# Sliding-window attention by pairs of chunks: one run of logits in six PSUM banks, and keys turned four chunks at a time by DMA

## The chip, the cores and the metric

The kernel runs on one core of one Trainium2 chip. The core has a matrix engine (TensorE, PE in the profile; PEld is its loading of the stationary operand), a vector engine (DVE), a scalar engine (ACT), GpSimd (POOL) and a queue engine (SP) that issues nearly all DMA transfers. TensorE writes to PSUM, which has eight banks of 128 partitions x 512 float32; DVE and ACT read them. The metric is the device time of one execution in microseconds (us); a kernel's time is the median of its runs.

## The reference

One layer of a hybrid decoder on x (2048 tokens x 1024 channels, float32). The tokens are cut into 16 chunks of 128.

```python
proj = einsum('bsd,de->bse', rms_norm(x, norm_w), w_in)      # 1024 -> 2816 columns
rq, rk, rv, rg, sq, sk, sv, sg = split(proj)                 # retention, then attention
ro = group_norm(retention(rotary(rq), rotary(rk), rv)) * silu(rg)
so = sliding_window_attention(sq, sk, sv, ...) * silu(sg)
x + einsum('bse,ed->bsd', concatenate([ro, so]), w_out)
```

The attention has 8 query heads and 2 key heads of 64 channels. Queries and keys are RMS-normed per head. A token attends to the 128 tokens up to itself, so a chunk of queries meets its own keys and those of the chunk before:

```python
logits = einsum('bnqhgd,bnkhd->bhgnqk', qb, kband) * HD ** -0.5
logits = where(mask, logits + bias, -1e30)                   # bias by distance and head
probs = softmax(concatenate([logits, sink]))[..., :-1]       # one learned sink per head
out = einsum('bhgnqk,bnkhd->bnqhgd', probs, vband)
```

The retention runs over the same chunks with a state that is passed on from chunk to chunk.

## The kernel before

*Products.* The two projections are four streams of block products (`products`, L754): three over columns of w_in (512, 384 and 512 wide), and one over w_out. A stream multiplies blocks by a scheme with seven products in place of eight for two-by-two blocks, for eight pairs of chunks: 56 products. A product is 12 matmuls into one bank ("acc"): each operand is split into a high and a low part in a faster format ("x" and "w"; `split`, L569), and three combinations of the parts are summed over four blocks of 128 rows. ACT makes the high part and DVE the low one. A finished product leaves its bank by a copy on ACT or an addition on DVE (tiles s, t, u, r, c).

*Attention* runs beside the second and third stream. `window` (L1188) goes through the chunks, and `attend` (L1323) does one of them. DVE scales queries ("qn") and keys ("kn"). The queries are turned by `turn_by_dma` (L484): ACT splits the 32-bit words into two planes of 16-bit halves ("apart"), SP stores them to DRAM ("planes_dram") and a transposing DMA brings them back turned ("qT"). The keys are turned by one transpose on TensorE against the identity ("ident,kn"), and ACT writes them, scaled, into "ks", a tile that holds the keys of a chunk, of the one before and of the one after, laid out so that a band of 160 keys is a contiguous slice. The logits of one head and 32 queries are one matmul of 64 rows x 32 columns against 160 keys; a chunk has 32 of them (eight heads by four groups of 32 queries), each of which the profile counts as two matmuls, so 64, in two operations of 32 counted matmuls, each with two banks (L1384 to 1397). DVE adds bias and finds the row's extreme ("lg<-m,bias,nsnk", two for a bank), ACT takes the exponential and its sum, and DVE turns the weights in blocks of 32 x 32 ("pT<-lg"). `values` (L1227) multiplies them with the values for two chunks at once, 144 counted matmuls of 32 x 64 into four banks, which ACT copies out ("so").

*Retention* (L907) follows with 17 steps of matmuls of 64 x 64, and the gates and the fourth stream after it.

*What sets the order.* Nothing here is ordered by hand. Every operation is recorded with its engine, an assumed duration and a due time (`Program.op`, L147). `emit` (L176) then runs a list scheduler: it keeps a clock for each engine, picks the operation that can start first and breaks ties by due time, and fixes the order of each engine's instructions. Because one helper records all of them, nearly every row of the profile has line L421, and the tiles' names tell the operations apart. Due times count products: stream 1 is 0 to 56, stream 2 is 56 to 112 and so on. Chunk c's attention is due at `WIN[0] + c * WIN[1]`, retention's at `RET`, the gates' at `GATE`. The planner has costs for a change of tile size on TensorE (`CHANGE`, `LESSER`), for the fetch of its instructions (`PIECE`, `ASKED`, `LONG`), and limits: `CAP` (buffers of each kind; "bank" is 8), `SHARE` (buffers for each use; block products may take 3 banks, everything else 6), `AHEAD` and `AHEAD_OF` (how early a load, or the split of an x or w block, may be issued). `HELD` lists intermediate tiles that stay in SBUF and are neither stored to DRAM nor loaded again; `TURNED` lists the chunks whose tiles are turned by DMA.

The two operations of logits for one chunk:

```python
for t in range(2):
    ...
    op(f32(160, 2), go, [qT, ks_t], pls[2 * t : 2 * t + 2], due + 0.5 + 0.3 * t, "eighths", label="logits", many=64)
```

Of the kernel before, what the change touches and what calls it, by code (L numbers as in the profile page):

```python
# [39 lines left out]
P = 128  # L40
# [63 lines left out]
LATER, CROWD, MOST, SOONER = 0.5, 0.0, 7, 62.0  # L104
# [239 lines left out]
HELD = {"sums": ((3, 1), (5, 4), (5, 5), (6, 3), (6, 6), (7, 0), (7, 1), (7, 5)), "ro": (1, 4, 8, 9, 10, 12, 13, 14, 15), "q": (0, 3, 13, 14), "gates": (1, 7), "so": (2, 14, 15)}  # L344
# [49 lines left out]
VALUES = {"T": (2.26, 2.48, False)}  # L394
# [30 lines left out]
def layer(ctx, tc, xt, xfirst, xtok, nw, w_in, w_rn, qkw, sinks, biasg, rope, decays, dmask, gpow, w_out, out):  # L425
# [113 lines left out]
    planes_dram = [scratch([P, 1024], f"planes{n}_dram", NCH, U16) for n in range(4)]  # L539
# [648 lines left out]
    def window(at):  # L1188
# [22 lines left out]
        ks_t = kb("ks", "att")  # L1211
        op({"G": (0.3, 0.4, True)}, lambda e: e.memset(ks_t()[:, 0:P], 0.0), [], [ks_t], at(0) - 4, label="no keys")
        held = []
        for c in range(NCH):
            i = c >= 2 * FIRST_PAIRS
            a, b = held_q.get(c), sb("akv", [P, P])
# [3 lines left out]
            load(b, aq_dram[1][c], at(c) - 4, 64, of=lambda t: t[:, :P])  # L1220
            fac = Part(qk_batches[i][1], lambda t, k=c - 2 * FIRST_PAIRS * i: t[:, k, :])
            held.append(attend(c, a, b, fac, qk_batches[i][1], at(c), bias_t[c > 0], ks_t, nsnk))
            if c % 2:
                values(c - 1, held, at(c))
                held = []

# [47 lines left out]

    def qk_sums(p, row, col, b, due):
# [47 lines left out]
    def attend(c, a, b, fac, facs, due, bias_t, ks_t, nsnk):  # L1323
        slot = c % 2
        qn, kn = kb("qn", "att"), sb("kn", [P, P])
# [9 lines left out]
        if c in HELD["q"] and c in TURNED["q"]:  # L1335
# [4 lines left out]
        op(  # L1340
            {"V": (0.22, 0.3, True)},
            lambda e: e.tensor_tensor(
                kn().rearrange(hd, d=HD), b().rearrange(hd, d=HD), fac()[:, 8:10].unsqueeze(2).to_broadcast([P, KVH, HD]),
                ALU.mult,
            ),
            [b, facs], [kn], due, label="kn",
        )

        pk, pq = ps(), ps()
        op(  # L1350
            turns(1), lambda e: e.transpose(pk()[:, 0:P], kn(), ident()), [kn, ident], [pk], due + 0.2, "small",
            label="turn k", many=2,
        )
# [13 lines left out]
        def go(e):  # L1367

            b4 = ks_t().rearrange("p (b t) -> p b t", t=P)
            e.activation(  # L1370
                b4[:, 1:3, :] if slot == 0 else b4[:, 0:4:3, :],
                pk()[:, 0:P].unsqueeze(1).to_broadcast([P, 2, P]), AF.Copy,
                scale=wqk(),
            )

        op({"A": act(256, 0.09)}, go, [pk, wqk], [ks_t], due + 0.3, label="ks")


        if c % SUMMED == 0:
            sums_of[:] = [sb("nm", [P, SUMMED, AH]), sb("den", [P, SUMMED, AH]), [], []]  # L1380
        nm, den, nms, dens = sums_of
        lgs = [wide("lg") for _ in range(KVH)]

        pls, weights_of = [ps() for _ in range(4)], {}  # L1384
        for t in range(2):

            def go(e, t=t):
                for j in range(2):
                    for u, q in enumerate(QUARTERS):
                        for g, r in enumerate((L, H)):  # L1390
                            o = (2 * t + j) * P + u * 32
                            e.matmul(
                                pls[2 * t + g]()[q, j * 160 : j * 160 + 160], qT()[r, o : o + 32],
                                ks_t()[r, slot * 256 + u * 32 : slot * 256 + u * 32 + 160], start=True, stop=True,
                            )

            op(f32(160, 2), go, [qT, ks_t], pls[2 * t : 2 * t + 2], due + 0.5 + 0.3 * t, "eighths", label="logits", many=64)
        for bank, heads in enumerate([(2 * t + j, g) for j in range(2)] for t in range(2) for g in range(2)):
            later, n = due + 0.5 + 0.2 * bank, len(heads)
            pl, g = pls[bank], heads[0][1]  # L1400
            lg = lgs[g]
            out = Part(lg, lambda t, i=heads[0][0]: t[:, i * 160 : (i + 2) * 160])

            part = lambda x, k=bank: x[:, c % SUMMED, k // 2 * 4 + k % 2 : k // 2 * 4 + 4 : 2]
            nmp, denp = Part(nm, part), Part(den, part)
            nms.append(nmp)
            dens.append(denp)

            def go(e, pl=pl, out=out, heads=heads):
                for j, (i, g) in enumerate(heads):  # L1410
                    h, o = 2 * i + g, slice(j * 160, j * 160 + 160)
                    e.tensor_tensor_reduce(
                        out()[:, o], pl()[:, o], bias_t[i]()[:, g * 160 : g * 160 + 160],
                        1.0, nsnk()[:, h : h + 1], ALU.add, ALU.min, nm()[:, c % SUMMED, h : h + 1],
                    )

            op(
                {"V": (0.312 * n, 0.312 * n + 0.13, False)}, go, [pl, nsnk, *(bias_t[i] for i, _ in heads)], [out, nmp],
                later, label="bias", also=(nm, lg),
            )  # L1420

            def go(e, out=out, heads=heads):
                for j, (i, g) in enumerate(heads):
                    h, o = 2 * i + g, slice(j * 160, j * 160 + 160)
                    e.activation(
                        out()[:, o], out()[:, o], AF.Exp, scale=-1.0, bias=nm()[:, c % SUMMED, h : h + 1],
                        accum_out=den()[:, c % SUMMED, h : h + 1],
                    )

            op(  # L1430
                {"A": (0.417 * n, 0.417 * n + 0.14, False)}, go, [out, nmp], [out, denp], later + 0.2, "exp", label="exp",
                also=(nm, den, lg),
            )
            weights_of[bank] = out
        pTs = []
        for g in range(KVH):
            if slot == 0:
                wholes[g] = wide("pT")
# [144 lines left out]

WIN = (58.5, 4.8)
RET = (124.5, 2.15)
GATE = (139.0, 5.65)

LEAD = 7.0  # L1590


_SHAPES = {
# [92 lines left out]
```

## Time and profile before

| | us |
|---|---|
| median of three runs (676.03 to 679.65) | 676.88 |
| the profiled execution | 673.99 |
| its span | 672.2 |
| TensorE busy | 663.9 |
| DVE busy | 589.9 |
| ACT busy | 475.6 |
| logits matmuls, 1024, summed | 21.7 |
| values matmuls, 1152, summed | 26.5 |
| key transposes on TensorE, 16, summed | 4.1 |

Matmuls are pipelined, so the busy time of a group and the duration of one of its members say little of what it costs on the path; that is read from the starts of the work around it, in order of time. Rows of that view have the start, the time to the end of the last of a row, the engine, the line, the operation, the tiles written and read, the array's tile size, the shape and the count; "[0.58 <-ACT ks L421]" is idle time before the row and what ended it. In a view by stretches the columns are the stretch, its length, the busy time of PE, PEld, DVE, ACT and POOL with the number of instructions, the granted TensorE clock, the busy share of the DMA engines and GB/s.

### The profile page before, as it was taken

What the parts mean: (1) busy time and instruction counts of PE and PEld (TensorE: products, weight loads), DVE (VectorE), ACT (ScalarE), POOL (GpSimd) and SP (SyncE); (2) the same over time, 40 slices, a digit from 0 to 9 for tenths busy, and PEclk for the clock granted to TensorE, in tenths of its full rate; (3) what the DMA queues carried; (4) which work ended last, traced back from release to release, by engine and by line L of the source; (5) the groups of instructions that cost most, each with busy time, mean ns of one, the idle gap of its engine ahead of it and who ended that gap; (6) DMA issues with size and microseconds to landing.
All of it is one profiled execution on the core that took longest, in us unless ns stands there. A gap on an engine that the chain in (4) does not pass through costs nothing.

```text
span 672.2 us, 16349 instructions
## 1 busy us (share of the span) xinstructions
PE 663.9 (99%) x5948; PEld 560.2 (83%) x5948; DVE 589.9 (88%) x1369; ACT 475.6 (71%) x1147; POOL 16.7 (2%) x39
## 2 busy tenths in 40 slices
PE   9999999999999999999999999999999999999998
PEld 7888888889999999898887777688888888888886
DVE  6999967887899978899998998989998999987782
ACT  7662788657898764889889987989999844533300
POOL 0000000034100000000000000000000000000000
PEclk9999999999999999999999999999999999999999
DMA  8976699988887999999989887989998685025652
GB/s 315 362 245 228 190 363 301 334 281 293 239 205 214 284 240 280 321 274 325 262 227 255 209 259 232 257 257 226 275 260 245 192 201 198 1 79 196 213 186 95
DMA packets 154144, 161.65 MB, mean 240 GB/s; under 512 B 67792, under 2 KB 95312, under 8 KB 154064
## 3 DMA queue, kind: packets, MB, share of 16 engines
q1 hardware_dynamic: 153920, 160.60, 79.5%
q8 instruction: 47, 0.77, 0.5%
q14 instruction: 33, 0.27, 0.1%
q10 hardware_dynamic: 144, 0.00, 0.0%
HBM read 97.05 MB, written 49.35 MB: 218 GB/s over the span
## 4 chain that ended last, share of the span: by engine, by line
PE 87%; DMA 4%; DVE 4%; ACT 3%; issue 1%; SPq 1%; ACTq 0%; DVEq 0%
PE acc L421 79%; PE m L421 8%; DMA planes_dram<-apart 2%; SPq L421 1%; DVE w L421 1%; DVE x L421 1%; DMA x<-s_dram 1%; DMA w<-in_w_in 0%; DMA ro_dram<-ro 0%; DMA g_dram<-c 0%; ACT qk L421 0%; ACT so L421 0%; ACT ro L421 0%; ACT apart L421 0%; DVE state L421 0%
## 5 line engine op out<-in xcount | busy, mean ns | idle before, releaser
L421 PE MATMUL acc<-w,x 128*128 128x512 f32 (+1 forms) x2700 | 591.5, 377 | 1.8 <-DVE x L421 0.9
L421 PEld LDWEIGHTS acc<-w,x 128*128 128x128 f32 x2700 | 491.5, 188 | 88.5 <-issue 6.0
L421 DVE TENSOR_TENSOR x<-x 128x512 fp32r<-128x512 f32 (+2 forms) x220 | 143.4, 672 | 15.8 <-ACT x L421 12.7
L421 ACT ACTIVATE x<-x 128x512 fp32r<-128x512 f32 (+1 forms) x187 | 111.3, 617 | 29.9 <-DVE x L421 16.7
L421 DVE TENSOR_TENSOR w<-w 128x512 fp32r<-128x512 f32 (+3 forms) x96 | 61.1, 656 | 3.4 <-ACT w L421 3.3
L421 ACT ACTIVATE lg<-lg,nm 128x160 f32<-128x160 f32 x128 | 53.1, 421 | 6.8 <-DVE nm L421 6.7
L421 ACT ACTIVATE w<-w 128x512 fp32r<-128x512 f32 (+1 forms) x72 | 40.9, 603 | 14.0 <-DVE w L421 4.0
L421 DVE SCALAR_TENSOR_TENSOR w<-w,nw_sb 128x512 fp32r<-128x512 f32 (+3 forms) x72 | 49.8, 704 | 1.1 <-ACT w L421 1.0
L421 DVE TENSOR_TENSOR s<-acc,s 128x512 f32<-128x512 f32 (+1 forms) x64 | 41.5, 649 | 8.9 <-PE acc L421 8.6
L421 DVE CUSTOM_DVE_ANT_0 lg<-m,bias,nsnk 128x160 f32<-128x160 f32 x128 | 40.4, 379 | 0.9 <-PE m L421 0.9
L421 DVE TENSOR_TENSOR t<-acc,t 128x512 f32<-128x512 f32 (+2 forms) x33 | 21.0, 638 | 13.2 <-PE acc L421 13.2
L421 ACT ACTIVATE x<-go 128x512 fp32r<-128x512 f32 x27 | 16.6, 629 | 18.1 <-PE acc L421 5.8
L421 DVE TENSOR_TENSOR r<-acc,t 128x512 f32<-128x512 f32 (+1 forms) x32 | 20.9, 653 | 9.7 <-PE acc L421 8.7
L421 ACT ACTIVATE w<-w,nw_sb 128x512 fp32r<-128x512 f32 (+3 forms) x42 | 27.1, 681 | 2.5 <-DMA w<-in_w_in 2.4
L421 DVE TENSOR_TENSOR t<-acc,s 128x512 f32<-128x512 f32 (+1 forms) x32 | 20.8, 650 | 8.8 <-PE acc L421 6.7
L421 ACT ACTIVATE s<-acc 128x512 f32<-128x512 f32 (+1 forms) x32 | 18.4, 575 | 12.5 <-PE acc L421 10.5
L421 DVE STREAM_TRANSPOSE pT<-lg 128x640 f32<-128x640 f32 x32 | 26.2, 831 | 0.2
L421 ACT ACTIVATE apart<-qn 128x1024 uint16<-128x1024 uint16 x16 | 16.9, 1063 | 12.7 <-DVE qn L421 5.5
L421 ACT ACTIVATE ro<-ro,nmu,rg 128x128 f32<-128x128 f32 x64 | 25.1, 481 | 0.0
L421 ACT ACTIVATE ro<-m 64x256 f32<-64x256 f32 (+2 forms) x54 | 21.5, 398 | 4.8 <-DMA planes_dram<-apart 3.8
L421 ACT ACTIVATION_READ_ACCUMULATOR lg<-lg,nm 128x1 f32 x128 | 24.6, 192 | 0.0
L421 PE MATMUL m<-pT,vn 32*64 32x128 f32 (+1 forms) x1152 | 21.8, 285 | 1.4 <-ACT ro L421 1.0
(146 smaller groups left out, 592.7 us busy)
## 6 DMA issues: line engine op xcount, KB each, us to landing
x<-in_xt SPq DMA_DIRECT2D x80, 256.0 KB, 4.5
planes_dram<-apart SPq DMA_DIRECT2D x54, 256.0 KB, 3.2
x<-s_dram SPq DMA_DIRECT2D x48, 256.0 KB, 3.9
w<-in_w_in SPq DMA_DIRECT2D x40, 256.0 KB, 4.9
xk<-in_xtok SPq DMA_DIRECT2D x32, 256.0 KB, 4.3
res<-in_xtok SPq DMA_DIRECT2D x32, 256.0 KB, 3.3
s_dram<-x SPq DMA_DIRECT2D x24, 256.0 KB, 4.1
w<-in_w_out SPq DMA_DIRECT2D x20, 256.0 KB, 3.8
```

Source lines behind the costliest of these rows:

```text
L421: return lambda *a, **k: self.order.put(op(*a, **k))
```

## The change

Three things.

1. *Logits by pairs.* `attend` is split in two. `turned` does what belongs to one chunk (scaling, turning, writing the keys). The new `attend` takes a pair of chunks and records one operation of 128 counted matmuls that writes six banks, three for each key head, with three, three and two slices of 160 columns. There are two "ks" tiles, used in turn by pairs; the keys of a pair's second chunk are written into this pair's tile and into the next one's. Bias and exponential are recorded by bank: three, three or two at once. The "lg" buffers become four.
2. *Keys by fours.* From chunk 4 on, `turned_keys` loads the keys of four chunks as one tile (256 KB with a stride), scales them in one DVE operation of 512 columns, and turns them by `turn_by_dma`. Chunks 0 to 3 keep their own load of 64 KB, scaling and transpose on TensorE.
3. *Orders planned anew.* The planner's limits, due times, assumed durations and lists change: which tiles are held, which are turned by DMA, and how early what may be done.

```diff
-CAP = {"k": 83, "lg": 3, "pT": 2, "vn": 1, "bank": 8}
+CAP = {"k": 83, "lg": 4, "pT": 2, "vn": 1, "bank": 8}
-SHARE = {"x": 8, "raw": 57, "acc": 54, "wr": 49, "wh": 18, "att": 54, "ret": 35, "rin": 61, "gate": 6, "mix": 28, "norm": 5, "res": 3, "turned": 12, "vn": 3, "first": 5, "block": 3, "rest": 6}
-AHEAD_OF = {"x": 2.5, "wh": 7.5}
-AHEAD, SPARE, SPARED = 14.5, 4, ("raw", "wr")
+SHARE = {"x": 20, "raw": 83, "acc": 96, "wr": 22, "wh": 29, "att": 27, "ret": 38, "rin": 75, "gate": 18, "mix": 89, "norm": 5, "res": 5, "turned": 23, "vn": 3, "first": 5, "block": 3, "rest": 6}
+AHEAD_OF = {"x": 4.5, "wh": 4.0}
+AHEAD, SPARE, SPARED = 16.5, 4, ("raw", "wr")
-LATER, CROWD, MOST, SOONER = 0.5, 0.0, 7, 62.0
+LATER, CROWD, MOST, SOONER = -0.5, 2.0, 24, -288.0
-HELD = {"sums": ((3, 1), (5, 4), (5, 5), (6, 3), (6, 6), (7, 0), (7, 1), (7, 5)), "ro": (1, 4, 8, 9, 10, 12, 13, 14, 15), "q": (0, 3, 13, 14), "gates": (1, 7), "so": (2, 14, 15)}
-TURNED = {"q": range(NCH), "qk": range(NCH), "gated": (0, 2, 4, 7, 8, 13)}
-EARLIER_Q, EARLIER_K = 0.0, 11.0
-SCALED = (1.0, 2.75)
+HELD = {"sums": ((3, 6), (5, 0), (5, 5), (6, 2), (6, 3), (6, 4), (6, 7), (7, 0), (7, 3), (7, 7)), "ro": (2, 3, 6, 7, 8, 10, 12, 15), "q": (1, 5, 8, 12, 15), "gates": (0, 3, 4, 6), "so": (2, 8, 13)}
+TURNED = {"q": range(NCH), "k": range(4, NCH), "qk": range(NCH), "gated": (2, 3, 6, 7, 8, 11)}
+EARLIER_T = 2.0
+EARLIER_Q, EARLIER_K = 11.5, -1.5
+SCALED = (3.5, 5.6)
-VALUES = {"T": (2.26, 2.48, False)}
+VALUES = {"T": (2.46, 2.66, False)}
-WIN = (58.5, 4.8)
-RET = (124.5, 2.15)
-GATE = (139.0, 5.65)
-LEAD = 7.0
+WIN = (65.0, 3.6)
+RET = (116.5, 1.85)
+GATE = (138.5, 7.0)
+LEAD = 3.5
...
+    def turned_keys(c, due):
+        t, kT, i = kb("k4", "att"), kb("kT", "att"), c >= 2 * FIRST_PAIRS
+        soon, facs = due - EARLIER_T, qk_batches[i][1]
...
+            e.tensor_tensor(k, k, facs()[:, o : o + 4, 8:10].unsqueeze(3).to_broadcast([P, 4, KVH, HD]), ALU.mult)
+        op(both(512), go, [t, facs], [t], soon, label="kn")
+        turn_by_dma(t, kT, planes_dram[4][c // 4], soon + 0.1)
+        return kT
...
-        op({"A": act(256, 0.09)}, go, [pk, wqk], [ks_t], due + 0.3, label="ks")
+        here, there = ks_t[c // 2 % 2], ks_t[1 - c // 2 % 2]
+        if c % 2 == 0:
...
+            op({"A": act(256, 0.05)}, go, [pk_of, wqk], [here], due + 0.3, label="ks")
+        else:
+            for t, o in ((here, 3 * P), (there, 0)) if c < NCH - 1 else ((here, 3 * P),):
...
-        pls, weights_of = [ps() for _ in range(4)], {}
-        for t in range(2):
...
-            op(f32(160, 2), go, [qT, ks_t], pls[2 * t : 2 * t + 2], due + 0.5 + 0.3 * t, "eighths", label="logits", many=64)
+        lgs = {(k, g): wide("lg") for k in range(2) for g in range(KVH)}
+        pls = {(g, b): ps() for b in range(3) for g in range(KVH)}
+        where = {(k, i): ((k * GRP + i) // 3, (k * GRP + i) % 3) for k in range(2) for i in range(GRP)}
+        def go(e):
+            for (k, i), (b, j) in where.items():
+                for u, q in enumerate(QUARTERS):
+                    for g, r in enumerate((L, H)):
+                        o = i * P + u * 32
+                        e.matmul(
+                            pls[g, b]()[q, j * 160 : j * 160 + 160], qTs[k]()[r, o : o + 32],
+                            ks_t()[r, k * 256 + u * 32 : k * 256 + u * 32 + 160], start=True, stop=True,
+                        )
+        op(f32(160, 8), go, [*qTs, ks_t], [*pls.values(), free_of.of.setdefault(c0 // 2, Buf(ap=()))], due + 0.5, "eighths", label="logits", many=256)
...
+                    {"V": (0.306 * n, 0.306 * n + 0.13, False)}, go, [pl, nsnk, *dict.fromkeys(bias)], outs + nmps,
...
```

More of the change, by code (lines that the diff above doesn't have):

```diff
@@ L538, in layer @@
     so_dram = scratch([P, 512], "so_dram", NCH)
-    planes_dram = [scratch([P, 1024], f"planes{n}_dram", NCH, U16) for n in range(4)]
+    planes_dram = [scratch([P, 1024], f"planes{n}_dram", NCH, U16) for n in range(5)]
     def rsqrt(eng, y, x, n, due, yb, xb, tag, cost=None):
@@ L1380, in attend @@
+        return qT
+    def attend(c0, qTs, ks_t, due, bias_t, nsnk):
+        if c0 % SUMMED == 0:
             sums_of[:] = [sb("nm", [P, SUMMED, AH]), sb("den", [P, SUMMED, AH]), [], []]
         nm, den, nms, dens = sums_of
-        lgs = [wide("lg") for _ in range(KVH)]
-        pls, weights_of = [ps() for _ in range(4)], {}
-        for t in range(2):
[L1387 to L1395, printed above, removed]
-            op(f32(160, 2), go, [qT, ks_t], pls[2 * t : 2 * t + 2], due + 0.5 + 0.3 * t, "eighths", label="logits", many=64)
@@ L1398, in attend @@
[L1398 to L1434, printed above, removed]
@@ new lines, in attend @@
+        held = []
+        for k in range(2):
+            pTs = []
+            for g in range(KVH):
+                lg = lgs[k, g]
+                if k == 0:
+                    wholes[g] = wide("pT")
+                pT = Part(wholes[g], lambda t, k=k: t[:, k * 640 : k * 640 + 640])
+                op(
+                    {"V": (0.76, 0.85, False)}, lambda e, lg=lg, pT=pT: e.transpose(pT(), lg()), parts_of[k, g], [pT],
+                    due + 1.3 + 0.3 * g + 0.6 * k, label="turn weights", also=(lg, wholes[g]),
+                )
+                pTs.append(pT)
+            held.append(pTs)
```

127 lines of the change are left out of this document (86 added, 41 removed).

## The prediction

> **What bounds the kernel now.** I read the page's head first, then the busy time by stretches, then TensorE's own waits, and last TensorE's instructions in order of time.
>
> ```profile
> span 672.2 us, 16349 instructions
> PE 663.9 (99%) x5948; PEld 560.2 (83%) x5948; DVE 589.9 (88%) x1369; ACT 475.6 (71%) x1147; POOL 16.7 (2%) x39
> ...
> PE 87%; DMA 4%; DVE 4%; ACT 3%; issue 1%; SPq 1%; ACTq 0%; DVEq 0%
> ```
>
> ```profile
> 280.00:336.00 56.00, 56.00 (x786) 48.72 (x786) 55.97 (x150) 48.52 (x149) 0.00 (x0) 1.00 1.02 293
> ...
> 168.00:560.00 392.00, 388.16 (x4717) 330.24 (x4716) 362.10 (x966) 331.14 (x846) 2.74 (x5) 1.00 0.90 249
> ```
>
> TensorE is busy for 99% of the span, and the chain that ended last is TensorE's for 87%. So the time is the sum of what TensorE executes, plus its few stalls. The second fence (columns: PE, PEld, DVE, ACT, POOL, granted clock, DMA share, GB/s) has the stretch in which attention and retention run beside the products: DVE has 362.10 of 392 us there, 92%, and between 280 and 336 us it is full (55.97 of 56). The clock is 1.00 throughout. A change pays in full if it takes work from TensorE, and only as far as DVE, second in line, keeps up.
>
> What TensorE itself waited for, all in all (total, times, longest):
>
> ```profile
> PE m L421 <- ACT ro L421: 1.0, 2, 0.6
> PE acc L421 <- DVE x L421: 0.9, 2, 0.5
> PE m L421 <- ACT ks L421: 0.6, 1, 0.6
> PE acc L421 <- ACT x L421: 0.5, 1, 0.5
> PE m L421 <- issue: 0.5, 2, 0.2
> PE acc L421 <- DVE t L421: 0.3, 1, 0.3
> ```
>
> That is 3.8 us of waits (beside 1.2 us at the very start, which the change does not touch). The loss is larger, because the work restarts from an empty pipeline:
>
> ```profile
> 418.65 0.62 PE L421 MATMUL m<-state,qkT 64*64 64x128 f32 x16
> 419.61 0.70 PE L421 MATMUL acc<-w,x 128*128 128x512 f32 x2 [0.34 <-DVE t L421]
> 420.72 2.59 PE L421 MATMUL acc<-w,x 128*128 128x512 f32 x10 [0.41 <-DVE x L421]
> 423.24 0.67 PE L421 MATMUL m<-v,sT 64*64 64x128 f32 x16
> ...
> 450.93 0.62 PE L421 MATMUL m<-state,qkT 64*64 64x128 f32 x16
> 454.42 0.67 PE L421 MATMUL m<-v,sT 64*64 64x128 f32 x16
> ```
>
> The same work took 423.24-418.65 = 4.59 us with 0.75 us of waits and 454.42-450.93 = 3.49 us without: 1.10 lost for 0.75 shown, 1.47 to 1. All the stalls together are then about 3.8 x 1.47 = 5.6 us.
>
> **The change, part by part.** *Longer logits runs (16 chunks in 17 runs become 8 runs).* TensorE in order (start, us, tile, count):
>
> ```profile
> 157.23 6.25 PE L421 MATMUL acc<-w,x 128*128 128x384 f32 x35
> ...
> 195.57 7.56 PE L421 MATMUL acc<-w,x 128*128 128x384 f32 x42
> 203.05 1.34 PE L421 MATMUL m<-ks,qT 64*32 64x160 f32 x64
> 204.33 8.60 PE L421 MATMUL acc<-w,x 128*128 128x384 f32 x48
> 212.85 2.53 PE L421 MATMUL m<-pT,vn 32*64 32x128 f32 x144
> 215.31 2.36 PE L421 MATMUL acc<-w,x 128*128 128x384 f32 x12
> 217.60 1.34 PE L421 MATMUL m<-ks,qT 64*32 64x160 f32 x64
> ...
> 237.83 2.46 PE L421 MATMUL m<-pT,vn 32*64 32x128 f32 x136
> 240.52 0.45 PE L421 MATMUL m<-pT,vn 32*64 32x128 f32 x8 [0.23 <-issue]
> 240.90 1.85 PE L421 MATMUL acc<-w,x 128*128 128x384 f32 x9
> 242.59 0.27 PE L421 MATMUL m<-ident,kn 128*128 128x128 f32 x1
> 242.61 2.33 PE L421 MATMUL acc<-w,x 128*128 128x384 f32 x12
> 244.87 1.34 PE L421 MATMUL m<-ks,qT 64*32 64x160 f32 x64
> ...
> 358.32 0.77 PE L421 MATMUL m<-ks,qT 64*32 64x160 f32 x32
> 359.02 2.33 PE L421 MATMUL acc<-w,x 128*128 128x512 f32 x9
> 361.29 0.77 PE L421 MATMUL m<-ks,qT 64*32 64x160 f32 x32
> ```
>
> A run of 64 takes 204.33-203.05 = 1.28 us from its first matmul to the next product; a run of 32 takes 0.70. Another 32 therefore cost 0.58, and 64 cost 0.12 of entry beside 1.16 of work. Undisturbed products follow each other at (6.25-0.34)/34 = 0.174 us (first row, less the last one's own 0.34). The 42 between 195.57 and 203.05 should take 7.31 us and took 7.48: another 0.17 for leaving one tile size and entering the next. Merging two runs saves 0.12 + 0.17 = 0.29; eight merges, 2.3 us. The one chunk that now runs in two halves (358.32, 361.29) saves its own entry and border as well, about 0.3.
>
> *Twelve of the 16 key transposes leave TensorE.* From 240.90 to 244.87 are 21 products and one transpose, 3.97 us. Twelve products between the same kinds of runs take 217.60-215.31 = 2.29, and nine more 1.57. The transpose costs 0.11, not its 0.27; twelve cost 1.3 us. Four stay, for the chunks whose keys aren't turned by DMA. Together TensorE's own work shrinks by 2.3 + 0.3 + 1.3 = 3.9 us, all on the path.
>
> *What the keys cost elsewhere.* Durations (min/median/max, ns), and the landing of what goes through the turned planes:
>
> ```profile
> L421 ACT ACTIVATE apart<-qn x16: 1046/1054/1134, 159.6 to 358.5; 128x1024 uint16<-128x1024 uint16 x16
> ...
> L421 SPq DMA_TRANSPOSE qT<-planes_dram x16: 1227/1366/3378, 167.8 to 372.6; - x16
> ...
> DMA to landing us min/median/max: 2.0/3.7/7.3
> ...
> L421 DVE TENSOR_TENSOR kn<-akv,fac x16: 280/284/533, 160.2 to 347.4; 128x128 f32<-128x128 f32 x16
> ```
>
> DVE loses twelve key scalings of 0.28 (3.4 us) and gains three four times as wide, 0.7 each by the width: about -1.3 us. ACT gains three splittings into planes at 1.05, and the odd chunks' keys are written in two steps rather than one; some 4 us of a queue that has 61 us free in the 392. SP issues three stores and three transposes (1.37 each) more and nine loads fewer; per group of four this is one more blocking wait on a splitting, and the loads queued behind it wait too. Bounds of that: 0 and the three transposes' own 4.1 us. I take 0, because the loads are placed up to 16.5 products ahead, some 35 us; without that lead the 4.1 us would stand on the path.
>
> The new wait is on the path of a logits run: scaling 0.7, splitting 1.05, store 3.7, transpose 3.7 and the masked copy, some 9.5 us where scaling, transpose and copy took one. The order puts products in that gap. If a landing comes at 7.3 instead of 3.7, the run and everything behind it on TensorE wait 3.6 us. Bounds for the three groups: 0 and 10.8; I take 0, since no row of TensorE's waits names a transfer, and keep 3.6 (one late) for the range.
>
> *Instruction fetch.* The values run at 237.83 shows a wait on "issue" and lasts 240.90-237.83 = 3.07 us, where the one at 212.85 lasts 2.46: 0.6 lost. The waits list has two such among eight runs of 288 instructions (matmul and weight load counted apart). No run of 128 lost any. The new logits runs have 256, nearest to the values. Bounds: 0 and 8 x 0.6 = 4.8; by two in eight, 1.2, which I take. [...]
>
> *Orders planned anew.* Kept sums, queries and gates become more, kept retention outputs fewer: four net, eight transfers of 256 KB less. DMA is at 0.90 of the stretch, so this relieves rather than loads. The split blocks x get 20 buffers instead of 8 and may be made 4.5 units ahead instead of 2.5. The waits "DVE x", "ACT x" and "DVE t" (0.9 + 0.5 + 0.3 = 1.7, by 1.47: 2.5 us) are products whose split block came late; with twice the lead I let them go. The waits on ro and ks (1.6, by 1.47: 2.4) stay: bank and key waits, of which the new order has as many. Bounds for the new order's stalls: 0 (gain 5.6) and twice as many (loss 5.6).
>
> **The sum.** -3.9 - 2.5 + 1.2 = -5.2 us. The profiled execution took 673.99 us (span 672.2 and 1.8 around it), 2.9 below the median of the three runs, 676.88; the difference is taken from either. 676.88 - 5.2 = 671.7 us.
>
> **The rivals.**
> *Six banks (slower).* The run writes six of eight banks and needs all six free at once, so the products have two while they drain. They drain through DVE only: 16 bias operations at 0.305 from start to start (40.4 us busy in 128, partly overlapping):
>
> ```profile
> L421 DVE CUSTOM_DVE_ANT_0 lg<-m,bias,nsnk 128x160 f32<-128x160 f32 x128 | 40.4, 379 | 0.9 <-PE m L421 0.9
> L421 DVE TENSOR_TENSOR s<-acc,s 128x512 f32<-128x512 f32 (+1 forms) x64 | 41.5, 649 | 8.9 <-PE acc L421 8.6
> L421 DVE STREAM_TRANSPOSE pT<-lg 128x640 f32<-128x640 f32 x32 | 26.2, 831 | 0.2
> ```
>
> With two banks, a product of 12 x 0.174 = 2.09 us runs while the other bank is evacuated (0.65). It stalls from 2.09-0.65 = 1.44 us of DVE work ahead of the evacuation, and two groups of three (1.8) are more. Two groups and a transpose ahead cost 0.92 x 2 + 0.83 + 0.65 - 2.09 = 1.2 us. Once per run is 10 us: 676.9 - 3.9 + 10 = 683. Attention is also asked for in 3.6 units a chunk, not 4.8, which packs this DVE work a third more densely into a stretch where DVE is already full. Against it: the order is laid out with DVE's costs, TensorE waited on the banks of before for 1.0 us in all, and x is now made further ahead. [...] Chance 0.19.
>
> *No gain.* TensorE does the 3.9 us less, but DVE, full at 280-336 and now fuller, or fetches in most of the eight runs (4.8), take it back: 676.9 - 3.9 + 4.8 = 677.8, or 675.4 with half. Chance 0.23.
>
> *All stalls gone.* 676.9 - 3.9 - 5.6 = 667.4, if the deeper lead cures the bank waits too. Chance 0.08.
>
> **How the numbers follow.** Half a per cent, 3.4 us, is about what a measurement of this kernel can tell from no change. The forecast has 0.50 and lies 5.2 below; with the stall-free case, faster is 0.58. The no-gain case is "same", 0.23; six banks is slower, 0.19. The forecast's own range is 667 to 673.5. For 8 in 10 it must reach into the slow case, up to 683, and at the low end to a little below the stall-free time: 666.
>
> **What would show it.** TensorE's logits in 8 runs of 128, each about 1.28 + 2 x 0.58 = 2.4 us; four transposes of kn; three more turned planes; waits on "DVE x" gone. If I am wrong, waits of products (acc) on evacuations (DVE s, t, r) within 10 us after a logits run would show the six banks, waits on "issue" inside logits the fetch, and waits on "ks" at chunks 4, 8 or 12 the late keys.

## The result, and the profile after

The changed kernel takes 685.6 us (median of four runs, 683.2 to 686.2), the kernel before 676.45 beside it: a ratio of 1.0124, with an interval of 1.0097 to 1.0151. So it is slower by about 9 us, where the prediction said 5 us faster. The profiled executions stand 12.2 us apart in span (684.4 and 672.2); that of before was one of its quick ones.

The page of the changed kernel, its head, and a view by stretches (columns as in the fence of the same stretches before):

```profile
span 684.4 us, 16323 instructions
...
PE 666.4 (97%) x5936; PEld 564.8 (83%) x5936; DVE 590.8 (86%) x1359; ACT 479.1 (70%) x1156; POOL 15.1 (2%) x39
```

```profile
280.00:336.00 56.00, 51.03 (x751) 46.32 (x750) 50.11 (x149) 43.47 (x150) 0.00 (x0) 0.97 0.88 258
168.00:560.00 392.00, 381.24 (x4667) 328.29 (x4666) 354.49 (x946) 324.81 (x840) 4.11 (x8) 0.98 0.91 245
```

TensorE now stands still for some 18 us of the span, where it was 8. DVE, which was full between 280 and 336 us, has 6 us free there. And the granted clock (third number from the right: 0.97, 0.98) is no longer 1.

What TensorE waited for in the changed kernel (total, times, longest):

```profile
PE acc L422 <- ACT s L422: 5.1, 3, 2.6
PE m L422 <- issue: 5.0, 2, 2.9
PE acc L422 <- ACT x L422: 2.5, 1, 2.5
...
PE m L422 <- DMA vn<-aq_dram: 0.5, 1, 0.5
PE acc L422 <- DVE r L422: 0.2, 1, 0.2
```

That is 13.3 us in 8 waits, beside 3.8 in 9 before. "DVE x" is gone, as predicted, and so are "ACT ro" and "ACT ks"; "ACT x" grew from 0.5 to 2.5 us. DVE stands in one row with 0.2 us: it is not what stops the products. New are few and long waits: on ACT (copies "s" and a split block "x") and on "issue". No row has "ks" in it, and the rows in order of time below have no wait inside a logits run.

TensorE in order of time, around each kind:

```profile
162.99 2.38 PE L422 MATMUL acc<-w,x 128*128 128x384 f32 x12 [1.17 <-ACT s L422]
166.74 14.83 PE L422 MATMUL acc<-w,x 128*128 128x384 f32 x84 [1.36 <-ACT s L422]
...
212.15 2.43 PE L422 MATMUL m<-ks,qT 64*32 64x160 f32 x128
214.50 11.72 PE L422 MATMUL acc<-w,x 128*128 128x384 f32 x66
...
274.04 2.26 PE L422 MATMUL acc<-w,x 128*128 128x384 f32 x6 [2.46 <-ACT x L422]
276.23 2.90 PE L422 MATMUL m<-ks,qT 64*32 64x160 f32 x128
279.07 3.24 PE L422 MATMUL acc<-w,x 128*128 128x384 f32 x17
...
297.46 2.26 PE L422 MATMUL m<-pT,vn 32*64 32x128 f32 x123
301.83 0.66 PE L422 MATMUL m<-pT,vn 32*64 32x128 f32 x21 [2.10 <-issue]
...
327.17 0.44 PE L422 MATMUL m<-pT,vn 32*64 32x128 f32 x5 [2.86 <-issue]
...
380.23 1.65 PE L422 MATMUL acc<-w,x 128*128 128x512 f32 x3 [2.58 <-ACT s L422]
```

Three mechanisms can be read here.

**Late places.** The rows of ACT just ahead of the three longest waits on it:

```profile
166.19 0.49 ACT L422 ACTIVATE s<-acc 128x384 f32<-128x384 f32 x1 [1.69 <-DMA planes_dram<-apart]
...
269.93 1.06 ACT L422 ACTIVATE apart<-qn 128x1024 uint16<-128x1024 uint16 x1 [1.97 <-DMA planes_dram<-apart]
...
379.58 0.60 ACT L422 ACTIVATE s<-acc 128x512 f32<-128x512 f32 x1 [1.78 <-DMA g_dram<-c]
```

A copy out of a bank waits for a store of something else. It needs no data from that store; it needs its place. The addresses in the built program show that the copy at 166.19 writes where an "apart" tile lay whose store to DRAM was still under way, that the splitting at 269.93 writes over the "apart" tile of the keys turned by fours, and that the copy at 379.58 writes over the "c" stored to g_dram. The three stores landed 4.8, 5.2 and 4.3 us after their issue, and ACT went on about 0.1 us after each. Behind the waiting copy stand the other ACT operations, and behind those the products. When ACT began to wait, three, four and eleven of the 83 places held no tile in use, by the last use of each tile in the trace. The planner counts a place as free 2.7 us after the store's turn on the bus. The list of transfers of the changed kernel has the median from issue to landing as its last number:

```profile
planes_dram<-apart SPq DMA_DIRECT2D x57, 256.0 KB, 3.4
...
kT<-planes_dram SPq DMA_TRANSPOSE x3, 6.0
```

The view of the tile "planes_dram" lists who waited for it (engine and tile, total, times), and the spread of its landings:

```profile
  ACT apart L422: 5.1, 3
  ACT x L422: 3.1, 1
  ACT s L422: 2.4, 2
...
DMA to landing us min/median/max: 2.1/4.0/7.3
```

**Instruction fetch.** Both waits on "issue" lie inside a values run, at instruction 5569 and 6337 of TensorE's 12,036. The trace has 47 packets of queue q8, kind "instruction", of 16,384 bytes each: 256 of the 12,036 to a packet. 5569 and 6337 are both 193 + a multiple of 256, and so are the numbers of the two waits on "issue" in the kernel before, 2241 and 3777; they are taken for the first instruction of a packet. To tell how late a packet starts, time is counted here from TensorE coming within 320 instructions of it. That mark is the planner's (`ASKED`); when a packet is asked for no run shows, but none in the traces of the changed kernel and of the one before started with more than 297 to go. The two packets started 8.3 and 7.5 us after the mark, and TensorE went on 1.2 and 1.5 us after each had arrived. The mean packet between 150 and 430 us starts after 3.8.

**Half clock.** At three of the standstills, or just behind, the granted clock falls to a half. A view by stretches of the changed kernel (the third number from the right is the clock):

```profile
274.00:277.40 3.40, 3.36 (x46) 2.79 (x54) 1.85 (x3) 2.20 (x7) 0.00 (x0) 0.52 0.86 262
...
327.00:332.00 5.00, 4.83 (x18) 3.71 (x19) 4.29 (x7) 3.79 (x11) 0.00 (x0) 0.66 0.68 215
...
380.00:386.80 6.80, 6.57 (x72) 5.16 (x73) 5.02 (x12) 6.74 (x16) 0.00 (x0) 0.52 0.87 245
```

The clock record has 3.41, 3.41 and 6.83 us at 0.5, 13.65 together, of which a half, 6.8 us, is lost at most: about 0.8 us of the 13.65 lie inside the standstills themselves, which leaves 6.4. It can be seen in the work: the logits run at 212.15 takes 2.35 us to the next product, the one at 276.23, partly at half clock, takes 2.84; four runs of retention between two products take 3.19 us in the last of the stretches (381.81 to 385.00) and 1.71 behind it (388.62 to 390.33).

So the two profiles differ like this. Before: 3.8 us of waits. After: 13.3 us of waits and 6.8 us of half clock. That is 16.3 us more; the span grew by 12.2, so the work itself shrank by some 4 us.

### The profile page after: what moved, and what is told of

Read it like the earlier page. It is cut to its first block, busy times and chain, and to the rows that moved or that the text cites. A ratio compares the mean times of both kernels' runs of the same rounds, so it can differ in the third digit from the quotient of the medians.

```text
span 684.4 us, 16323 instructions
## 1 busy us (share of the span) xinstructions
PE 666.4 (97%) x5936; PEld 564.8 (83%) x5936; DVE 590.8 (86%) x1359; ACT 479.1 (70%) x1156; POOL 15.1 (2%) x39
## 4 chain that ended last, share of the span: by engine, by line
PE 56%; DMA 2%; DVE 1%; issue 1%; ACT 1%; SPq 0%; ACTq 0%
PE acc L422 49%; PE m L422 8%; DMA planes_dram<-apart 1%; DMA qkT<-planes_dram 1%; DMA g_dram<-c 1%; ACT x L422 0%; DVE w L422 0%; DVE x L422 0%; DVE qk L422 0%; DVE r L422 0%; DVE st L422 0%; ACT s L422 0%; DVE tcos L422 0%; DVE k L422 0%; DVE tsin L422 0%
## 5 line engine op out<-in xcount | busy, mean ns | idle before, releaser
L422 PEld LDWEIGHTS m<-pT,vn 32*64 32x64 f32 x1152 | 19.3, 130 | 8.7 <-issue 7.3
L422 ACT ACTIVATE c<-acc 128x512 f32<-128x512 f32 (+1 forms) x24 | 13.4, 557 | 14.0 <-PE acc L422 12.7
L422 ACT ACTIVATE xk<-xk 128x512 f32<-128x512 f32 x32 | 19.8, 620 | 3.6 <-DVE w L422 1.8
```

What stands on the lines that cost most here:

```text
L422: return lambda *a, **k: self.order.put(op(*a, **k))
```

## The experiments

**1. Places chosen by what has landed.** The changed kernel, the order of every engine kept; only the place in SBUF that a tile gets is another one. The oldest free place is taken, and one whose last use was a transfer counts as free 3 us later:

```diff
+                b.safe = max(getattr(b, "safe", 0.0), o.end + (INFLIGHT if e == "Q" else 0.0))
+                if not b.left and b.tag == "k":
+                    PLACES.append((b.safe, b.place))
...
+INFLIGHT = 3.0
...
+        if b.tag == "k":
+            found = min(PLACES)
+            PLACES.remove(found)
+            b.place = found[1]
+            return sbuf.tile([P, 512], b.dtype, tag=f"k{b.place}", bufs=1, name=b.name)
```

> The changed kernel with every engine's order as it is; only the place in SBUF that a new 2 KB tile gets is chosen otherwise: the free place that has been free longest, where a place freed by a store counts as free 3 us later than the planner has it. Theory A (late places): in the changed kernel ACT's copies s<-acc and its splittings apart<-qn stand still because their tiles got places whose last store had not landed; so TensorE's waits on 'ACT s' (5.1 us) and 'ACT x' (2.5 us) go, and with them two of the three stretches at half clock (3.4 and 6.8 us long, 5.1 us lost): 685.6 - 12.7 = about 673. Theory B (instruction fetch): these waits don't matter and the 'issue' waits (5.0 us) stay: 685. Theory C (six banks and DVE are too slow for the order): 685, since no bank and no engine's order changes.

Measured: 675.97 us (673.0 to 681.6), ratio to before 1.0001 (0.9971 to 1.0030). What TensorE waited for, all of it but the start:

```profile
PE m L427 <- issue: 6.2, 4, 2.4
...
PE acc L427 <- DVE x L427: 0.5, 1, 0.5
PE acc L427 <- issue: 0.4, 1, 0.4
```

Every wait on ACT is gone, and of the three stretches at half clock (13.65 us) one of 3.41 is left, behind a wait on "issue". So late places, with the half clock that followed them, cost the changed kernel 9.6 us. The waits on "issue" stay, 6.6 us.

**2 and 3. The borders between blocks of instructions moved.** 54 matmuls of one column more in the warm-up shift all later instructions by 216 against the borders; once in the changed kernel, once with the places chosen as well:

```diff
+        for _ in range(54):
+            e.matmul(pw()[:, 0:1], none()[:, 0:P], none()[:, 0:1], start=True, stop=True)
```

> The changed kernel with 54 more matmuls of one column behind the warm-up matmuls, unknown to the planner: every engine's order stays, but the borders of TensorE's blocks of 256 instructions fall 216 instructions earlier in the work. The added matmuls themselves cost 3 us or less at the start. Theory B (instruction fetch): both waits on 'issue' inside values runs (5.0 us) go or move, and the stretch at half clock behind the second (1.7 us lost): 685.6 - 6.7 + 3 = about 682, with the waits on ACT unchanged. Theory A: waits on 'ACT s' and 'ACT x' stay, 7.6 us. Theory C: waits stay where they are in the work, 688.

> Both of the edits above. If A and B together are the whole loss, the waits on ACT, on 'issue' and all stretches at half clock in the middle are gone: 673 - 6.7 + 3 = about 669, below the kernel before (676.5). Theory C: 685 to 688.

Measured: 702.73 us (ratio 1.0381, 1.0328 to 1.0433) and 700.03 us (1.0388, 1.0306 to 1.0471). Two things missed. The added matmuls were costed at 3 us at most, an estimate that rested on no run, and took about 23: the warm-up's 116 records were busy for 26.6 us where the 8 of the changed kernel took 3.5. And the waits on "issue" did not go; they moved. In the second kernel's list of waits:

```profile
PE m L422 <- issue: 8.2, 3, 3.0
```

The third had 7.5 us in 4, one of them, 1.5 us, inside a logits run. So it is not those two borders that lay badly; with these other borders, other runs are caught. With the added 23 us taken off, the two come to about 680 and 677, too rough to say more.

**4. The choice of places in the kernel before.** The same edit, the order of before kept.

> The kernel before with the same choice of places, its order as it is. Theory A: it has few such waits (TensorE waited 0.5 us for ACT x and 1.0 for ACT ro), so it gains 0 to 2 us: 675 to 676.5. If the choice of places helps any order by the same amount, 664.

Measured: 671.8 us (671.6 to 672.05), ratio 0.9921 (0.9897 to 0.9945), more than expected. The kernel before had late places too. Its runs spread over 7 us (672.7 to 679.7 in twenty), these over 0.5, which suggests that part of its time hung on what had landed when (later kernels with chosen places spread by 0.5 to 4.5 us, so this is not general). With both mended in the same way, the changed kernel is still 4.2 us slower (676.0 and 671.8). So of the 9.2 us between the two kernels, 5.0 are late places (9.6 less 4.6). For the other 4.2, its waits on "issue" are 6.6 us against this row's 1.4:

```profile
PE m L426 <- issue: 1.4, 2, 0.8
```

**5. Thinner values runs.** Experiment 1 with three of the nine blocks of keys in each values run; the other six are left out:

```diff
-            for b in range(9):
+            for b in (0, 4, 8):
```

> The changed kernel with places chosen by what has landed (676.0 us), where each of the 8 runs of values computes only 3 of its 9 blocks of keys: 96 instructions of TensorE in place of 288, the order of every engine as before; the output is wrong by that. The work left out is 6 of 10 parts of 2.46 us, 8 times: 11.8 us. Theory (blocks of 256 instructions come late because two dense runs stand between the asking and the border): with 96 in place of 288 the 6.6 us of waits on 'issue' fall under 2 us and the stretch at half clock goes too, so 657 to 660 us. Rival (a late packet is late whatever TensorE does): the waits on issue stay at 5 us or more, 664 to 666 us. A second rival, that other engines' waits come up where TensorE has become quicker, shows as waits on ACT or DVE of more than 2 us.

Measured: 667.86 us (ratio 0.988, 0.983 to 0.993). The whole list of what TensorE waited for beside the start:

```profile
PE m L427 <- DVE x L427: 2.1, 1, 2.1
PE acc L427 <- DVE r L427: 1.6, 2, 0.9
...
PE m L427 <- DVE nm L427: 1.2, 1, 1.2
PE acc L427 <- DVE x L427: 0.8, 1, 0.8
PE m L427 <- DVE state L427: 0.7, 1, 0.7
PE acc L427 <- DVE t L427: 0.4, 1, 0.4
PE m L427 <- ACT so L427: 0.3, 1, 0.3
PE acc L427 <- ACT s L427: 0.3, 1, 0.3
```

No wait on "issue" is left and the clock is 1.0 in the middle: the fetch theory's sign is there. (Leaving instructions out also moves every later border; but in experiments 2 and 3 moving them alone did not take the waits away.) The time did not reach 657 to 660, for the second rival came true at once: a TensorE that got quicker in an order planned for a slower one waited 7.4 us for DVE and ACT. The thin runs also took 1.1 to 2.0 us rather than the 1.0 they were costed at.

The traces have the time that each border left between coming within 320 instructions and reaching it (less the wait on "issue" itself), and how long after that mark its packet started (27 to 31 borders between 150 and 430 us of each run):

| kernel | borders with under 8 us | mean start of a packet, us | packets that started after more than 7.4 us | waits on "issue", us |
|---|---|---|---|---|
| before | 5 | 3.5 | 0 | 0.5 |
| before, places chosen | 5 | 3.8 | 0 | 1.4 |
| changed | 10 | 3.8 | 4 | 5.0 |
| changed, places chosen | 10 | 4.3 | 4 | 6.6 |
| the same, thin values | 3 | 4.3 | 2 | 0.0 |

Two things go together. TensorE comes earlier: a logits run of 256 instructions (128 matmuls and as many loads of weights) in 2.4 us and a values run of 288 in 2.5 stand so close, it is argued from these counts, that more borders leave little time. And although the mean start is nearly the same, single packets are later: the two waits of the changed kernel are at borders that left 8.4 and 7.0 us, with packets that started after 8.3 and 7.5 and took 1.0 each. With thin values two packets are as late and no wait comes of it. Why single packets start after 7 to 9 us stays open: neither the number nor the bytes of the DMA packets under way at the mark go with it (correlations of 0.09 and 0.20 over the 92 packets of the changed kernel and the one before).

**6 to 8. The old and the new structure, each ordered again.** The choice of places, and longer times in the planner: 8.0 us for a block of instructions, a transfer seen 1.2 us later. Under these the planner's settings (due times, limits, lists of held and turned tiles) were searched anew, about as long for each kernel. In the changed kernel, cut:

```diff
-LATE = 0.7
+LATE = 1.2
-PIECE, FIRST, ASKED, LONG, MORE = 256, 193, 320, 5.5, 1.0125
+PIECE, FIRST, ASKED, LONG, MORE = 256, 193, 320, 8.0, 1.0125
-RET = (116.5, 1.85)
-GATE = (138.5, 7.0)
+RET = (117.0, 1.65)
+GATE = (136.0, 6.6)
```

The last of the three differs from the first by `TURNED = {..., "k": (), ...}` and an order of its own.

> The changed kernel with its structure kept, the choice of places of the earlier run, and its order planned anew for longer times: 8.0 us for a block of instructions in place of 5.5, a transfer seen 1.2 us later in place of 0.7, and the settings searched under these. Planner's own time 663.1 us (the changed kernel's own order comes to 669.5 under the same times). Theory (the loss was the order and its places, the TensorE work saved is real): 665 to 670 us, below the 671.8 of the kernel before with places chosen so; waits on issue at most 3 us, no stretch at half clock. Rival (denser runs of matmuls cost at the borders in any order): 673 us or more, with over 5 us of issue.

> Control: the kernel before with the same choice of places and its order searched as long under the same longer times. Planner's own time 666.4 us. Theory: the structure of the change is worth 3 to 4 us when both orders are made in the same way, so 668 to 673 us here, 3 to 4 above the changed kernel replanned. Rival (dense runs cost what they save): level with the changed kernel replanned within 1.5 us, or below it.

> Only the first part of the change: logits of two chunks in one run with six banks, the keys normed and turned chunk by chunk as before, the same choice of places, the order searched as long under the same longer times. Planner's own time 667.9 us. Theory: the merge alone gives 2.3 us of TensorE, the turning of keys 1.3: within 2 us of the old structure replanned and 1 to 5 us above the full change replanned. Rival (the transposing DMAs of keys crowd the queue): below the full change replanned.

Measured: 670.94 us (ratio 0.9915, 0.9879 to 0.995) for the full change, 673.22 (0.9958, 0.9935 to 0.9981) for the old structure, 676.63 (0.9995, 0.9972 to 1.0018) for the logits alone. The first two lie in the order that the theory had, but both just above their ranges (to 670 and to 673), and 2.3 us apart where 3 to 4 were expected; their single runs hardly overlap (669.4 to 672.2 and 671.4 to 675.9). The full change has 3.4 us of "issue" where 3 at most were expected, and a part of it lies inside a logits run:

```profile
215.47 0.46 PE L427 MATMUL m<-ks,qT 64*32 64x160 f32 x4 [1.21 <-issue]
```

The third missed: it is slower than the old structure, and its list has the fetch again,

```profile
PE m L427 <- issue: 5.9, 3, 2.2
PE acc L427 <- issue: 2.7, 1, 2.7
```

8.6 us of it, though its order too was planned for 8.0 us. One of its packets started only after 9.8.

**9 to 11. A second order, the keys alone, and still longer fetches.** The ninth has the full change, the times of the sixth and another order found under them. The tenth has the kernel before with `turned_keys` put in and nothing else of the change, ordered under the same times. The eleventh is the full change with `LONG = 9.5`.

> The changed structure with chosen places and another order found under the same longer times (8.0 us for a block of instructions, 1.2 us for a transfer to be seen). Planner's own time 661.7 us, against 663.1 for the order replanned earlier, which ran in 670.9. Theory (the structure of the change is worth something once places and fetches are provided for): the 7.8 us between plan and chip come again, so 667 to 671 us, below the kernel before with chosen places (671.8) and below the one replanned (673.2). Rival (the first replanned order was a lucky one): 672 us or more.

> Only the second part of the change: keys of four chunks normed at once and turned by transposing DMAs, the logits of each chunk in two operations with four banks as before; chosen places, the order searched as long under the same longer times. Planner's own time 664.6 us (666.4 for the old structure, 667.5 for the logits alone). Theory (runs of 256 instructions of logits beside the 288 of values make the waits on issue; the keys' part has none of them and takes 1.3 us from TensorE): under 2 us of issue, and 0 to 3 us below the old structure replanned, so 669 to 673 us. Rival (late keys, or a crowded queue): above 674 us, with waits on ks or on transfers.

> The changed structure with chosen places and an order that keeps 9.5 us for a block of instructions, more than the 8.4 + 1.0 us of the latest one seen. Planner's own time 666.4 us, 4.6 us more than with 8.0: what the order gives up for it. Theory (a wait on issue comes only where less time is left than the packet takes): no wait on issue over 0.5 us and no stretch at half clock; the time 667 to 671 us, level with the orders for 8.0, since what is gained at the borders was paid in the order. Rival (late packets lie also where 9.5 us are left): issue of 2 us or more again.

Measured: 664.4 us (663.8 to 665.4; ratio 0.9824, 0.9792 to 0.9857), 668.5 us (668.3 to 668.9; 0.9883, 0.9851 to 0.9916), and 672.72 us (0.9942, 0.992 to 0.9965). All that TensorE waited for beside the start, first in the ninth kernel, then in the tenth:

```profile
PE m L427 <- issue: 2.0, 1, 2.0
...
PE acc L427 <- issue: 0.2, 1, 0.2
```

```profile
PE acc L427 <- DVE x L427: 0.5, 2, 0.3
PE m L427 <- ACT ro L427: 0.3, 1, 0.3
```

The ninth is the quickest of all, 1.8% below the kernel before, with the structure that the change brought. It gained more than expected, and so differs by 6.5 us from the sixth, which has the same structure and the same times in the planner; the tenth was just below the expected range, with no wait on a key or on a border. The eleventh has no wait on "issue" left, as expected, but took 672.7 where 671 was the most expected: its order pays with 3.6 us of waits on ACT's copies:

```profile
PE acc L427 <- ACT so L427: 1.9, 1, 1.9
PE acc L427 <- ACT s L427: 1.7, 2, 1.2
```

In this one order, keeping time for the latest packet at every border cost more than the few late ones. (The 8.4 us that its expectation calls the latest was not: the eighth kernel had the packet after 9.8.)

In time alone the structure is not settled by these eight orders, all with chosen places: the full change took 676.0, 670.9, 664.4 and 672.7 us, the old structure 671.8 and 673.2, the keys alone 668.5 and the logits alone 676.6. One reordering of the old structure stands beside three of the new one.

**12. The ninth's order without the choice of places.** Same instructions, same order on each engine, places handed out as in the changed kernel.

> The same instructions in the same order on every engine as in the best order found (664.4 us), but with the places in SBUF handed out as in the changed kernel. Theory (late places cost what they happen to hit; choosing places gave 9.6 us in the changed kernel and 4.6 in the one before): 668 to 675 us, with waits on ACT of 1 to 3 us in TensorE's list that the chosen places do not have, and runs spread by 3 us or more in place of 1.6. Rival (the new order, planned for 1.2 us later landings, does not need the choice): within 1.5 us of 664.4.

Measured: 670.47 us (667.8 to 672.8; ratio 0.991, 0.9877 to 0.9943). The waits on ACT are back:

```profile
PE acc L422 <- ACT s L422: 3.2, 2, 2.6
```

The longest of them begins two engines away, in a row of DVE:

```profile
157.83 1.15 DVE L422 SCALAR_TENSOR_TENSOR w<-w,nw_sb 128x384 fp32r<-128x384 f32 x2 [3.26 <-DMA aq_dram<-t]
```

The "w" is written where a "t" lay whose store landed at 157.74 (the addresses in the built program again); "hs" on DVE, "x" and then "s" on ACT, and the product at 165.21 come behind it.

Choosing places was worth 9.6 us in the changed kernel, 4.6 in the one before and 6.1 here, and with it the runs of the kernel before and of the ninth spread over 0.5 and 1.6 us, without it over 7 and 5. (The changed kernel's, which kept its waits on "issue", still spread over 8.6, and four of the reordered kernels over 2.8 to 4.5.)

## Why the prediction was wrong

The forecast was 5 us faster; it came out 9 slower, and outside the range.

*TensorE's own work: right.* Runs of logits were put at 2.4 us and took 2.35 (212.15 to 214.50), with 128 in each; four transposes of kn are left:

```profile
L422 PE MATMUL m<-ident,kn x4: 271/271/271, 181.4 to 209.9; 128*128 128x128 f32 x4
```

The saving itself can be had from the profiles, as an estimate: take from each span its waits (the start's aside), 0.175 us for each of them (the restart: the prediction's two rows lost 1.10 for 0.75 shown in two waits), and half of the time at half clock.

| | span | waits, times | half clock | left |
|---|---|---|---|---|
| before | 672.2 | 3.8, 9 | 0 | 666.8 |
| before, places chosen | 670.2 | 2.1, 4 | 0 | 667.4 |
| before, ordered again | 670.1 | 2.6, 4 | 0 | 666.8 |
| keys alone | 666.6 | 0.8, 3 | 0 | 665.3 |
| logits alone | 675.9 | 9.0, 5 | 1.7 | 664.3 |
| changed | 684.4 | 13.3, 8 | 6.8 | 662.9 |
| changed, places chosen | 673.7 | 7.1, 6 | 1.7 | 663.8 |
| changed, ordered again (6, 9, 11) | 667.6, 663.6, 671.0 | 4.8, 2.2, 5.6 | 0 | 661.9, 661.0, 664.2 |
| the ninth's order, places not chosen (12) | 670.5 | 5.4, 8 | 0 | 663.7 |

The old structure leaves 667.0 on average, the new one 662.9: 4 us, where the prediction's sum had 3.9; the keys alone 1.7 (predicted 1.3), the logits alone 2.7 (predicted 2.6). How rough this is can be seen in the ninth and the twelfth, which execute the same instructions in the same order and leave 661.0 and 663.7. That all six values of the new structure lie below all three of the old one is clear; the 4 us are good to 2 or 3, and that they agree with 3.9 so closely is luck.

*Orders planned anew: the step that failed.* "The waits 'DVE x', 'ACT x' and 'DVE t' ... I let them go" and "The waits on ro and ks ... stay", with bounds of 0 and of twice the stalls of before. This is the step: the term took 1.7 us of waits away (2.5 with the restarts), and the run added 5.0 us of waits, "issue" aside, and half clock behind them. The waits "DVE x" and "DVE t" did go, and those on ro and ks, which were to stay, went too. Those that came in their place were of a kind that the prediction had no term for: a tile waits for its place. The bound "twice as many" (5.6 us) was taken from the old order's waits, and an order made anew need not resemble the old one: without "issue" the waits went from 3.3 to 8.3 us, of which 7.6 are waits on ACT. Choosing the places alone took 9.6 us off (experiment 1). The transfer was in the profile of before: the prediction's own fence has landings of 2.0/3.7/7.3 us for the planes, and the pool has 83 places, the "k" of `CAP`. The sentence "no row of TensorE's waits names a transfer" was true and was the wrong test: the transfer stands in ACT's rows, one step behind, and TensorE's list names ACT. The same view of before that lists who waited for "planes_dram" would have shown it:

```profile
  ACT ro L421: 3.8, 1
  ACT apart L421: 1.6, 2
  ACT x L421: 1.4, 2
```

*Instruction fetch: right in kind, too small, and at the wrong place.* 1.2 us were taken, with 4.8 as the bound; 5.0 was measured, 6.6 with the places chosen, and 8.6 in the kernel with the logits alone. In the changed kernel both waits lie in values runs and none in the new logits runs, which the prediction had counted eight times; in the other orders most lie in values runs, three in logits runs (third and sixth experiment) and a few in products. So the sum over runs was the wrong form. In the traces of the changed kernel and the one before, the four waits came at the borders whose packet arrived between 1.3 us before TensorE got there and 1.4 us after it; at the other 56 borders between 150 and 430 us it had arrived 1.6 us ahead or more, and there was none. In these two kernels it was the time left at a border that counted, and the lateness of single packets has no term yet. Ten of the fourteen kernels profiled here lost between 0.5 and 8.6 us to "issue".

*Half clock: not in the prediction.* Its view had a clock of 1.00 throughout, with no standstill longer than 0.6 us behind the start. In the changed kernel three single waits, of 2.46, 2.86 and 2.58 us, came with 3.41, 3.41 and 6.83 us at half clock, which cost up to 1.7, 1.7 and 3.4 us more; one of 2.10 came with none. It was 6.4 to 6.8 us, between the waits on ACT (7.6) and those on "issue" (5.0).

*Late keys and six banks: rightly at nothing, with one side effect.* No wait names ks though kT lands 6.0 us after its issue in the median; DVE had time to spare; no product waits for a bank within 10 us behind a logits run. But the keys' new stores hold places too: the splitting at 269.93 waited for one of them, and TensorE 2.46 us behind it, with a stretch at half clock. The rival that was slower gave 683 us, near the time measured, by a mechanism that was not there.

The sum as it should have been, from the profiles: -3.9 us of work, +9.5 of waits, less 0.2 for one restart fewer, +6.8 of half clock: +12.2, against 12.2 between the two spans (11.8 with 6.4 for the half clock). That it closes to a tenth is luck, since the terms are good to 2 or 3 us.

## What to carry to other kernels

Where buffers are handed out from a pool that is nearly full, look who waits for a *store*: a place whose store is still under way is no free place. Taking the one that has been free longest changes no engine's order, and made three orders 4.6 to 9.6 us faster here. A change that takes work from the critical engine also brings its dense instruction runs closer together, so cost the fetch by the time left at each border (under 8 us at ten of them here, where it was five) and not by the run. And judge a structure by what is left after its waits are taken off: here that estimate has it some 4 us ahead from the start, and it took another order and a choice of places for a time to show it (664.4 us against 676). Orders of the same structure differed by 8 us, twice what the structure is worth.

## What was not expected of the hardware

*The stretches at half clock begin on a grid.* In the clock record of the changed kernel the three in the middle begin 79, 95 and 110 times 3.413 us after its first entry (at 273.83, 328.44 and 379.64 us of the span, the first entry at 4.18), and last one, one and two of these. They came with standstills of 2.46, 2.86 and 2.58 us, while one of 2.10 brought none. Cut at the borders of this grid, TensorE's idle time in the changed kernel was 2.24, 2.14 and 2.00 us in the three windows of 3.413 us ahead of them; in any other window up to TensorE's last matmul it was 1.41 at most (the standstill of 2.10 falls into two, 1.41 and 0.69), and in the kernel before, whose clock was 1.00 over its span, 0.99 at most. The length of a standstill alone does not tell: one of 2.58 us in the twelfth brought no such stretch (its clock is 0.999 over 670.5 us, where 3.41 us at a half would make it 0.997). What decides was not shown, and what held the changed kernel's last stretch for a second window, with 0.6 us of idle time in the first, stays open.

*Single blocks of instructions start late:* 8.4 us after TensorE had come within 320 instructions of it at the latest in the changed kernel and 9.8 in the eighth experiment, where the means in the table above are 3.5 to 4.3; and in the changed kernel and the one before this does not go with the transfers under way (correlations of 0.09 and 0.20). What delays them was not found.

*One-column matmuls were not cheap:* 54 of them, two records each in the profile, made the warm-up 23 us longer (26.6 us in the second experiment, 3.5 in the changed kernel), about 0.2 us a record.
